# Softmax weights left unscaled until after the product with the values

## The chip, the cores and the metric

The kernel runs on one core of a Trainium2 chip. The metric is the device time of one launch in microseconds. Every operand is fp32.

## The reference, cut to what matters

Two small transformer models run one after the other on 256 tokens of width 1024, each with two layers. The change lies in the first model. Each of its layers projects the 256 tokens and 256 context tokens to queries, keys and values of 16 heads of 64 channels: 8 plain heads ("a", two key heads shared by four query heads each), 4 neighbourhood heads ("b", with a window and a bias on the token keys) and 4 differential heads ("c"). The token queries attend to 512 keys (tokens and context); in layer 0 the context queries also attend, to the 256 context keys. For a and b

```python
p = jax.nn.softmax(s, axis=-1)
out = p @ v
```

and for c, with two maps of scores for each head, half the channels each,

```python
p = jax.nn.softmax(s, axis=-1)
w = p[:, :, 0] - lam * p[:, :, 1]
out = rms_norm(w @ v, g_sub) * (1.0 - lam_init)
```

An output projection, a gated residual and a convolutional feed-forward network follow; then the second model, with attentions of its own that the change doesn't touch.

## The kernel before, in words

All matrix products with weights (`gemm`, `mm`, `mm1`, lines 265 to 303) split both operands into a rounded part and a rest (`weight`, lines 254 to 263, by ScalarE and VectorE; `split`, lines 305 to 307, called by `parts`) and take three products. Activations are kept with channels on the 128 partitions and tokens on the free axis, so a tile of 128 channels holds two heads.

`first_layer` (line 606) runs, in each of the two layers, eight attentions of two heads each: two of kind c, two of kind b, four of kind a (lines 683 to 694). `attend` (line 518) does one. For each of the two heads it takes steps: two steps for the two blocks of 128 token queries, with a score tile of 128 x 512, and, in layer 0 only (`with_ctx`), one step for both blocks of context queries, whose two halves of 256 keys share one tile. In a step `scores` (line 524) fills a PSUM tile from the matmul pool (five banks); kind c fills two, one for each map. `weigh` (line 484) makes weights of them: `soft` (line 473) takes the negated row maximum on VectorE (line 478) and the exponential with that bias on ScalarE, which also gives the row sum (line 480); then VectorE takes the reciprocal of the sum (line 488), and ScalarE multiplies the weights by it, row by row, as the scale of a copy (line 491). For kind c the second map goes through `soft` too, and VectorE adds it to the first, scaled by lambda over its sum (lines 494 to 498). TensorE transposes the four blocks of weights into a PSUM tile of the other pool (three banks; lines 551 and 569), VectorE copies them to SBUF (lines 554 and 572), and after both heads the products with the values sum up the output, 64 channels of each head on its half of the partitions (lines 579 and 586). Here queries lie on the free axis and channels on the partitions, so that a factor for each query would have to lie along the free axis.

The output, still in PSUM, is split by `parts` (ScalarE line 306, VectorE line 307) for the output projection, for kind c after a norm (`subln`, lines 589 to 598).

Between the weights and their transposes each step calls `fill` (line 399), which puts in one tile of the projections still to be done (twelve tiles in each layer: in layer 0 the attentions of kind c use them up, in layer 1 the next ones use the last of them) or, after these, one step of the modulation weights' products (line 372).

The order of the instructions on each engine is fixed before the run by a planner, which takes the program's order as priority and puts an instruction forward where it expects its engine to be free and its inputs ready; buffers of a pool are handed out in that order. At run time each engine works its own list in order and waits at semaphores. The temporaries of 128 x 544 (`self.t`) are a pool of nine, the small columns (`self.s`) one of sixteen.

## Time and profile before

| | before |
|---|---|
| runs shown, median (lowest to highest) | 2435.0 us (2427.2 to 2436.84) |
| the profiled execution's own time | 2433.39 us |
| its span in the profile | 2431.6 us |
| mean granted clock of TensorE | 0.98 of full |
| TensorE products busy | 2320.8 us |
| VectorE busy | 1523.2 us |
| ScalarE busy | 1270.2 us |

All of the profile's numbers come from that one execution; 1.8 us of its time lie around the span. Times in the profile count from the span's start. Engines are PE (TensorE's products), PEld (its weight loads, which overlap the products), DVE (VectorE), ACT (ScalarE), POOL (GpSimd) and SP (SyncE). A busy TensorE isn't TensorE at its peak, since products overlap in its pipeline. "n_t<-at_t" names the tiles that an instruction writes and reads: `mm_t` and `at_t` are the two PSUM pools, `t_t` temporaries, `s_t` small columns, `n_t` activations, `q_t` queries, keys and values. A group may be followed by the idle time of its engine just before it and by the instruction that ended most of that.

### The profile page before, as it was taken

The page shows a single profiled execution, that of the slowest core. Times are in us where ns is not written, and L with a number is a line of the kernel's source. Part 1 is how long each engine was busy: PE and PEld are TensorE (multiplying, and loading weights), DVE is VectorE, ACT ScalarE, POOL GpSimd, SP SyncE. Part 2 cuts the span into 40 slices and gives each one's busy share as a digit, 9 for nine tenths or more (in the row PEclk, how much of TensorE's full clock was granted, in tenths as well). Part 3 has the DMA queues.
Part 4 walks back from the last instruction along what each step waited for, and adds up shares of the span by engine and source line. Part 5 has one row for each costly group of instructions (what it writes and reads, how often), then busy time and mean ns, then how long its engine had stood idle before and what let it go on. Part 6 is the DMA issues. An engine that isn't in the chain of part 4 may idle for free. (4 is left out here: it accounts for less than half of the span.)

```text
span 2431.6 us, 40872 instructions
## 1 busy us (share of the span) xinstructions
PE 2320.8 (95%) x16128; PEld 2043.5 (84%) x16128; DVE 1523.2 (63%) x2605; ACT 1270.2 (52%) x2196; POOL 401.7 (17%) x417
## 2 busy tenths in 40 slices
PE   5999999999999989999999999899999999998998
PEld 3665677778877758999999988899989999888997
DVE  4667665444547776776664876676466557666664
ACT  3658644333346775664444545554454444466553
POOL 0300021000022001211111320321121122113111
PEclk8999999999999999999999999999999999999999
DMA  7313335433233246556555533445545545334653
GB/s 269 103 37 131 113 130 173 139 121 96 93 117 120 71 156 211 194 177 191 183 168 180 167 106 105 148 157 174 174 148 178 169 147 195 104 114 149 196 180 118
DMA packets 100993, 358.57 MB, mean 147 GB/s; under 512 B 11488, under 2 KB 12864, under 8 KB 100544
## 3 DMA queue, kind: packets, MB, share of 16 engines
q1 hardware_dynamic: 98640, 349.82, 44.4%
q0 software_dynamic: 1792, 5.53, 0.9%
q8 instruction: 127, 2.08, 0.4%
q10 hardware_dynamic: 368, 0.59, 0.1%
q14 instruction: 66, 0.54, 0.1%
HBM read 354.83 MB, written 1.07 MB: 146 GB/s over the span
## 5 line engine op out<-in xcount | busy, mean ns | idle before, releaser
L269 PE MATMUL mm_t<-n_t,hi_t 128*128 128x272 f32 (+2 forms) x3600 | 1112.4, 310 | 25.4 <-ACT n_t L839 18.7
L270 PE MATMUL mm_t<-n_t,hi_t 128*128 128x272 f32 (+2 forms) x3600 | 1109.5, 308 | 6.0 <-DVE n_t L840 5.0
L271 PE MATMUL mm_t<-n_t,lo_t 128*128 128x272 f32 (+2 forms) x3600 | 1106.0, 308 | 1.1 <-DVE lo_t L262 1.1
L262 DVE TENSOR_TENSOR lo_t<-raw_t,hi_t 128x1024 fp32r<-128x1024 f32 (+1 forms) x574 | 713.2, 1246 | 391.2 <-ACT hi_t L261 387.1
L261 ACT ACTIVATE hi_t<-raw_t 128x1024 fp32r<-128x1024 f32 (+1 forms) x574 | 595.5, 1039 | 680.6 <-PE mm_t L270 509.4
L269 PEld LDWEIGHTS mm_t<-n_t,hi_t 128*128 128x128 f32 x3600 | 686.0, 191 | 77.7 <-ACT n_t L839 20.9
L270 PEld LDWEIGHTS mm_t<-n_t,hi_t 128*128 128x128 f32 x3600 | 688.5, 191 | 38.1 <-DVE n_t L840 8.4
L271 PEld LDWEIGHTS mm_t<-n_t,lo_t 128*128 128x128 f32 x3600 | 687.9, 191 | 33.0 <-issue 5.8
L269 PE MATMUL mm_t<-q_t,hi_t 128*128 128x272 f32 (+2 forms) x896 | 274.6, 307 | 0.7 <-ACT q_t L306 0.7
L270 PE MATMUL mm_t<-q_t,hi_t 128*128 128x272 f32 (+2 forms) x896 | 274.4, 306 | 0.0
L271 PE MATMUL mm_t<-q_t,lo_t 128*128 128x272 f32 (+2 forms) x896 | 274.3, 306 | 0.0
L343 POOL TENSOR_TENSOR t_t<-t_t 128x272 f32<-128x272 f32 (+1 forms) x108 | 122.9, 1143 | 540.2 <-ACT t_t L339 515.2
L269 PEld LDWEIGHTS mm_t<-q_t,hi_t 128*128 128x128 f32 x896 | 168.4, 188 | 8.8 <-ACT q_t L306 1.1
L270 PEld LDWEIGHTS mm_t<-q_t,hi_t 128*128 128x128 f32 x896 | 168.9, 188 | 7.6 <-DVE q_t L307 0.2
L271 PEld LDWEIGHTS mm_t<-q_t,lo_t 128*128 128x128 f32 x896 | 168.9, 189 | 7.5
L888 POOL TENSOR_TENSOR t_t<-t_t 128x272 f32<-128x272 f32 (+1 forms) x88 | 75.6, 860 | 443.3 <-DVE t_t L882 386.9
L738 POOL TENSOR_TENSOR t_t<-t_t 128x512 f32<-128x512 f32 (+1 forms) x44 | 56.7, 1288 | 442.2 <-ACT t_t L737 442.2
L882 DVE TENSOR_TENSOR t_t<-mm_t,t_t 128x272 f32<-128x272 f32 (+1 forms) x176 | 75.6, 436 | 64.2 <-PE mm_t L271 62.4
L372 PE MATMUL at_t<-raw_t,CS 128*32 128x256 f32 x768 | 70.6, 431 | 35.7 <-DMA raw_t<-in_w_ada_dram 35.4
L307 DVE TENSOR_TENSOR q_t<-t_t,q_t 128x272 fp32r<-128x272 f32 (+2 forms) x112 | 55.8, 498 | 73.4 <-ACT q_t L306 73.4
L306 ACT ACTIVATE q_t<-t_t 128x272 fp32r<-128x272 f32 (+2 forms) x112 | 52.3, 467 | 90.4 <-POOL t_t L738 47.8
L480 ACT ACTIVATE t_t<-mm_t,s_t 128x512 f32<-128x512 f32 (+1 forms) x120 | 72.7, 607 | 26.5 <-DVE s_t L478 25.7
(253 smaller groups left out, 2146.9 us busy)
## 6 DMA issues: line engine op xcount, KB each, us to landing
raw_t<-in_w_up_dram SPq DMA_DIRECT2D x264, 512.0 KB, 3.3
raw_t<-in_w_in_dram SPq DMA_DIRECT2D x118, 512.0 KB, 3.4
raw_t<-in_w_ada_dram SPq DMA_DIRECT2D x96, 512.0 KB, 4.4
raw_t<-in_w_dn_dram SPq DMA_DIRECT2D x96, 448.0 KB, 3.3
raw_t<-in_w_dn_dram SPq DMA_DIRECT2D x48, 512.0 KB, 3.6
raw_t<-in_w_out_dram SPq DMA_DIRECT2D x32, 512.0 KB, 3.4
raw_t<-in_w_fg_dram SPq DMA_DIRECT2D x16, 512.0 KB, 3.3
q_t<-cum POOLq DMA_DIRECT2D x8, 272.0 KB, 7.4
```

Source lines behind the costliest of these rows:

```text
L261: nc.scalar.activation(hi[:, :k], raw[:, :k], AF.Copy)
L262: nc.vector.tensor_tensor(lo[:, :k], raw[:, :k], hi[:, :k].bitcast(F32), ALU.subtract)
L269: self.nc.tensor.matmul(ps, wh, xh, start=start, stop=False)
L270: self.nc.tensor.matmul(ps, wh, xl, start=False, stop=False)
L271: self.last_mm = self.nc.tensor.matmul(ps, wl, xh, start=False, stop=stop).ins
L307: self.nc.vector.tensor_tensor(lo, src, hi.bitcast(F32), ALU.subtract)
L343: st.eng.tensor_tensor(st.acc, st.acc, sq, ALU.add)
L372: self.last_ada = nc.tensor.matmul(ps[32 * g:32 * g + 32], self.CS[:, k, :], wv[:, g], start=k == 0, stop=k == KC - 1).ins
L480: nc.scalar.activation(pm[:, i * nk:(i + 1) * nk], sp[:, i * nk:(i + 1) * nk], AF.Exp, bias=m[:, i:i + 1], accum_out=sm[:, i:i + 1])
L738: nc.gpsimd.tensor_tensor(u, u, g, ALU.mult)
L882: nc.vector.tensor_tensor(u, ps, z[0], ALU.mult)
L888: nc.gpsimd.tensor_tensor(u, u, g, ALU.mult)
```

## The change

The weights are no longer scaled in a step. A tile of eight columns, `sums`, collects the row sums of all steps of an attention: four for each head, the first two for the token queries, the others for the context queries. Kind c scales the second map by lambda times the first map's sum over the second's, so that the first map's sum stays as a common factor. After the steps of both heads VectorE takes the reciprocals (two instructions), and TensorE lays them along the free axis: for each block of 128 queries and each head a product of the column, repeated 64 times as weights, with the identity puts the reciprocals of 128 queries on the 64 partitions of that head, in one PSUM tile of the matmul pool. ScalarE copies that tile to SBUF, and after the products with the values VectorE multiplies the output with it into a temporary, which goes on to `parts` or `subln` in place of the PSUM tile. The second model's attention (`fox`) is as before.

```diff
--- before.py
+++ after.py
@@ -470,32 +470,30 @@
         self.evac(o[:, :n], tp[:, :n])
         return o
 
-    def soft(self, sp, nseg, nk):
+    def soft(self, sp, nseg, nk, sm):
 
         nc = self.nc
         pm = self.t()
-        m, sm = self.s(nseg), self.s(nseg)
+        m = self.s(nseg)
         nc.vector.tensor_reduce(m, sp.rearrange("p (s k) -> p s k", s=nseg), AX.X, ALU.max, negate=True)
         for i in range(nseg):
             nc.scalar.activation(pm[:, i * nk:(i + 1) * nk], sp[:, i * nk:(i + 1) * nk], AF.Exp, bias=m[:, i:i + 1],
                                  accum_out=sm[:, i:i + 1])
-        return pm, sm
-
-    def weigh(self, sps, nseg, nk, lam):
-
-        nc = self.nc
-        pm, sm = self.soft(sps[0], nseg, nk)
-        nc.vector.reciprocal(sm, sm)
-        for i in range(nseg):
-            u = slice(i * nk, (i + 1) * nk)
-            nc.scalar.activation(pm[:, u], pm[:, u], AF.Copy, scale=sm[:, i:i + 1])
+        return pm
+
+    def weigh(self, sps, nseg, nk, lam, sm):
+
+
+        nc = self.nc
+        pm = self.soft(sps[0], nseg, nk, sm)
         if len(sps) == 2:
-            pm1, sm1 = self.soft(sps[1], nseg, nk)
-            nc.vector.reciprocal(sm1, sm1)
-            nc.vector.tensor_scalar(sm1, sm1, lam, None, ALU.mult)
+            f = self.s(nseg)
+            pm1 = self.soft(sps[1], nseg, nk, f)
+            nc.vector.reciprocal(f, f)
+            nc.vector.scalar_tensor_tensor(f, f, lam, sm, ALU.mult, ALU.mult)
             for i in range(nseg):
                 u = slice(i * nk, (i + 1) * nk)
-                nc.vector.scalar_tensor_tensor(pm[:, u], pm1[:, u], sm1[:, i:i + 1], pm[:, u], ALU.mult, ALU.add)
+                nc.vector.scalar_tensor_tensor(pm[:, u], pm1[:, u], f[:, i:i + 1], pm[:, u], ALU.mult, ALU.add)
         return pm
 
     def stack(self, o, n, keys):
@@ -520,6 +518,9 @@
         nc = self.nc
         ident = self.con("ident")
         pts = []
+
+        sums = self.s(8)
+        nq = 4 if with_ctx else 2
 
         def scores(sp, hh, i, qs, ks, last):
 
@@ -544,7 +545,7 @@
                             nc.tensor.matmul(sp[:, rr * P:(rr + 1) * P], self.con("rev"), bias(qi, rr, hh), start=False,
                                              stop=rr == 1)
                     sps.append(sp)
-                pm = self.weigh(sps, 1, 512, lam)
+                pm = self.weigh(sps, 1, 512, lam, sums[:, 4 * hh + qi:4 * hh + qi + 1])
                 self.fill(l)
                 tp = self.atp()
                 for kc in range(4):
@@ -561,7 +562,7 @@
                         scores(sp[:, qi * 256:(qi + 1) * 256], hh, i, slice(256 + qi * P, 256 + (qi + 1) * P),
                                slice(256, 512), True)
                     sps.append(sp)
-                pm = self.weigh(sps, 2, 256, lam)
+                pm = self.weigh(sps, 2, 256, lam, sums[:, 4 * hh + 2:4 * hh + 4])
                 self.fill(l)
                 tp = self.atp()
                 for kc in range(2):
@@ -571,6 +572,16 @@
                 pcx = self.n()
                 nc.vector.tensor_copy(pcx, tp)
             pts.append((px, pcx))
+        for hh in range(2):
+            nc.vector.reciprocal(sums[:, 4 * hh:4 * hh + nq], sums[:, 4 * hh:4 * hh + nq])
+
+        rb = self.mmp()
+        for i in range(nq):
+            for hh in range(2):
+                nc.tensor.matmul(rb[64 * hh:64 * hh + 64, i * P:(i + 1) * P],
+                                 sums[:, 4 * hh + i:4 * hh + i + 1].to_broadcast([P, 64]), ident, start=i == 0, stop=i == nq - 1)
+        rs = self.t()[:, :nq * P]
+        nc.scalar.activation(rs, rb[:, :nq * P], AF.Copy)
         po = self.atp()
         for kc in range(4):
             for hh, (px, pcx) in enumerate(pts):
@@ -584,7 +595,9 @@
                     r0 = 64 * hh
                     vv = v[:, (2 + kc) * P + r0:(2 + kc) * P + r0 + 64]
                     nc.tensor.matmul(po[r0:r0 + 64, 256:512], vv, pcx[:, kc * 256:(kc + 1) * 256], start=False, stop=kc == 1)
-        return po[:, :512 if with_ctx else 256]
+        o = self.t()[:, :nq * P]
+        nc.vector.tensor_tensor(o, po[:, :nq * P], rs, ALU.mult)
+        return o
 
     def subln(self, po, n, gain):
         nc = self.nc
```

## Rows read from the trace of the kernel before

**Rows 1.** Page, part 1: busy us, share of the span, instructions of each engine.

```profile
PE 2320.8 (95%) x16128; PEld 2043.5 (84%) x16128; DVE 1523.2 (63%) x2605; ACT 1270.2 (52%) x2196; POOL 401.7 (17%) x417
```

**Rows 2.** Busy time by stretch: start:end, length, then each engine's us (instructions).

```profile
core 0: us, PE busy (x) PEld busy (x) DVE busy (x) ACT busy (x) POOL busy (x), PEclk, DMA share, GB/s
82.00:202.00 120.00, 112.37 (x506) 77.33 (x505) 81.45 (x167) 78.12 (x160) 21.39 (x24) 0.99 0.17 49
202.00:284.00 82.00, 73.87 (x551) 44.63 (x550) 66.33 (x156) 72.93 (x172) 1.41 (x2) 0.98 0.52 180
284.00:300.00 16.00, 16.00 (x91) 12.21 (x92) 5.71 (x15) 5.23 (x14) 0.00 (x0) 1.00 0.00 2
760.00:833.00 73.00, 67.77 (x360) 48.32 (x359) 54.80 (x114) 50.41 (x100) 17.61 (x19) 1.00 0.30 94
833.00:870.00 37.00, 31.39 (x226) 25.43 (x225) 26.10 (x69) 31.97 (x72) 5.68 (x8) 0.91 0.09 26
870.00:918.00 48.00, 47.42 (x345) 30.35 (x346) 33.78 (x90) 30.66 (x65) 0.00 (x0) 0.99 0.63 211
```

**Rows 3.** The same view of the first two attentions after the differential ones.

```profile
202.00:238.40 36.40, 32.80 (x271) 20.12 (x269) 29.00 (x67) 35.23 (x81) 1.41 (x2) 1.00 0.57 203
```

**Rows 4.** The same view, of line 491 alone.

```profile
core 0: us, ACT busy (x), PEclk, DMA share, GB/s
...
202.00:284.00 82.00, 24.03 (x42) 0.98 0.52 180
...
833.00:870.00 37.00, 4.94 (x7) 0.91 0.09 26
870.00:918.00 48.00, 11.97 (x17) 0.99 0.63 211
```

**Rows 5.** Timeline, 267.5 to 270.7 us: start, length, instruction [idle before, releaser].

```profile
267.53 0.68 ACT L480 ACTIVATE t_t<-mm_t,s_t 128x512 f32<-128x512 f32 x1
...
268.40 0.68 DVE L307 TENSOR_TENSOR n_t<-at_t,n_t 128x512 fp32r<-128x512 f32 x1
...
269.00 0.74 DVE L554 COPY n_t<-at_t 128x256 f32<-128x256 f32 x2
...
269.66 0.15 DVE L488 RECIPROCAL s_t<-s_t 128x1 f32<-128x1 f32 x1
...
269.85 0.72 ACT L491 ACTIVATE t_t<-t_t,s_t 128x512 f32<-128x512 f32 x1 [1.54 <-DVE s_t L488]
...
270.62 0.66 PE L551 MATMUL at_t<-CON,t_t 128*128 128x128 f32 x4 [1.53 <-ACT t_t L491]
```

**Rows 6.** Groups by form, whole span: busy us, mean ns | idle before, releasers.

```profile
L491 ACT ACTIVATE t_t<-t_t,s_t 128x512 f32<-128x512 f32 x64 | 45.2, 717 | 15.8 <-DVE s_t L488 15.6
...
L491 ACT ACTIVATE t_t<-t_t,s_t 128x256 f32<-128x256 f32 x32 | 14.6, 502 | 4.0 <-DVE s_t L488 3.9
...
L551 PEld LDWEIGHTS at_t<-CON,t_t 128*128 128x128 f32 x256 | 30.6, 146 | 21.0 <-ACT t_t L491 10.6 <-issue 7.5 <-ACT t_t L480 0.8
...
L579 PE MATMUL at_t<-n_t,q_t 128*64 128x256 f32 x256 | 36.6, 387 | 1.7 <-DVE n_t L554 1.3 <-DVE q_t L359 0.3
...
L544 PE MATMUL mm_t<-n_t,CON 128*128 128x128 f32 x64 | 9.9, 274 | 0.0
```

**Rows 7.** Timeline of TensorE, 264.2 us.

```profile
264.18 1.95 PE L579 MATMUL at_t<-n_t,q_t 128*64 128x256 f32 x16
```

**Rows 8.** Groups by form, 870 to 918 us.

```profile
L491 ACT ACTIVATE t_t<-t_t,s_t 128x512 f32<-128x512 f32 x17 | 12.0, 719 | 6.1 <-DVE s_t L488 5.9
...
L307 DVE TENSOR_TENSOR n_t<-at_t,n_t 128x256 fp32r<-128x256 f32 x5 | 2.1, 422 | 5.8 <-ACT n_t L306 5.8
...
L306 ACT ACTIVATE n_t<-at_t 128x256 fp32r<-128x256 f32 x5 | 1.9, 383 | 7.2 <-PE at_t L579 7.2
```

**Rows 9.** Groups by form, ScalarE, 202 to 284 us.

```profile
L306 ACT ACTIVATE n_t<-at_t 128x512 fp32r<-128x512 f32 x4 | 2.4, 592 | 1.3 <-PE at_t L586 1.3
```

## The prediction

> **What bounds the kernel now.** I read the page's engine shares first [rows 1]. Over the whole span TensorE has 95% busy, VectorE 63% and ScalarE 52%, which looks as if work taken off ScalarE could buy nothing. But the shares are an average, and all that the diff touches lies in the first model's two attention stages. So the second view is the busy time by stretch [rows 2]: layer 0's differential attentions (82 to 202 us), its neighbourhood and plain attentions (202 to 284), its end under the output projection (284 to 300), and for layer 1 the same at 760 to 833, 833 to 870 and 870 to 918. The reader should see two stretches in which ScalarE is the fuller of the two elementwise engines: 72.93 of 82 us (89%) at 202 to 284, and 31.97 of 37 (86%) at 833 to 870. In the first two attentions of the former it is 35.23 of 36.4 us, 97% [rows 3]. In the stretches of the differential attentions projections run between the steps and TensorE has 94 and 93% [rows 2]; there ScalarE has a third of its time free. At 284 to 300 TensorE has no gap at all.
>
> The third view is the scaling instruction by itself [rows 4]: 24.03 us of ScalarE at 202 to 284, 4.94 at 833 to 870, 11.97 at 870 to 918; the remaining 18.9 of its 59.8 us (45.2 + 14.6, [rows 6]) lie where TensorE is nearly full. The fourth is one step in order of time [rows 5]. The exponential ends at 268.21; its reciprocal is queued on VectorE behind a subtraction and two copies and starts at 269.66; the scaling runs 269.85 to 270.57; the transposes start at 270.62, and TensorE has stood idle for 1.53 us. So the detour sits in the chain of every step, and costs its own 0.15 and 0.72 us plus a place in VectorE's queue. Over the kernel ScalarE idles 19.5 us (15.6 + 3.9) for that reciprocal, and the weight loads of the four-block transposes 10.6 us for the scaling [rows 6].
>
> **What is removed.** The 96 scalings go: 64 of 512 columns at 717 ns and 32 of 256 at 502 ns [rows 6]. So do 80 reciprocals (6 in each attention of layer 0, 4 in layer 1) at 0.15 us [rows 5], 12.0 us of VectorE; I share them out over the stretches as the scalings are. In the differential attentions the second sum's reciprocal stays, and the small multiply by lambda becomes a small multiply by lambda and the first sum, 20 for 20. I cost that at nothing, because the operand that it adds, the first map's sum, is there before the second map's.
>
> **What is added, per attention (16).** (1) Two reciprocals of four or two columns, 0.15 us each like the others: 32, 4.8 us. (2) Broadcast products: 8 in layer 0, 4 in layer 1, 96 in all, 128 columns moving, 64 output rows, two row halves. No row shows one. The nearest is the product with the values, also 64 wide, with 256 columns: 16 take 1.95 us back to back [rows 7], 0.122 each, so half the columns give 0.061, 5.9 us in all. The other end is 0.274 us, a 128-column product by its whole duration [rows 6], 26 us in all. I take 0.061, because these too come in alternating halves. (3) One ScalarE copy out of PSUM, 0.383 us at 256 columns and 0.592 at 512 by the first split, which reads the same kind of tile [rows 8, 9]: 7.8 us. (4) One VectorE multiply, 0.68 us at 512 columns [rows 5] and 0.42 at 256 [rows 8], by the second split: 8.8 us. (5) One more tile of the five matmul banks and two more of the nine temporaries for a few us; as the temporary of every step falls free one scaling sooner, I cost it at nothing. Nothing moves on SyncE's or GpSimd's queue, and no DMA is added.
>
> So ScalarE loses 52.0 us net, VectorE gains 1.6 (8.8 + 4.8 - 12.0), TensorE gains 5.9.
>
> **The sum, by stretch.** *202 to 284* (five attentions end in it). ScalarE: 72.93 - 24.03 + 5 x 0.59 = 51.9 us. VectorE: 66.33 - 4.8 + 10 x 0.15 + 5 x 0.68 = 66.4. VectorE becomes the fuller one. If the stretch runs at the 89% that its fullest engine reaches now, it takes 66.4 / 0.89 = 74.6 us: 7.4 gained. Ends: at the 97% of [rows 3], 68.5 us, 13.5 gained; if VectorE stays at its present 81%, nothing. I take 7.4, because part of VectorE's idle time is waiting for what comes late as in [rows 5].
> *833 to 870* (one ends). ScalarE 31.97 - 4.94 + 0.38 = 27.4, VectorE 26.10 - 1.0 + 0.3 + 0.42 = 25.8; 27.4 / 0.864 = 31.7: 5.3 gained, between 0 and 8.8 (at 97%).
> *870 to 918* (five end). Neither engine is full (30.66 and 33.78 of 48), so only the chain shortens. ScalarE idles 5.9 us there ahead of its 17 scalings [rows 8]; I take half, 3, between 0 and 5.9.
> *82 to 202 and 760 to 833* (two end in each). TensorE's idle time is 7.6 and 5.2 us, which are the upper ends; 0 is the lower. What is removed lies beside projections; I take 1.5 each.
> *284 to 300* (one ends). TensorE is full: 0 gained.
> Gross gain 18.7 us. The broadcast products cost nothing at 202 to 284 and 833 to 870, where TensorE has gaps; elsewhere there are 52 of them (16, 8, 8 and 20), 3.2 us at 0.061, at most 14.2 at 0.274. At a layer's end the last output gets one VectorE operation more (0.42 to 0.68 us), but its last step is shorter by reciprocal and scaling (0.87): nothing.
>
> Net 15.5 us, from the profiled execution's own 2433.39 us: 2418. The median of the runs shown, 2435.0, is 1.6 us above it, so I predict **2420 us**.
>
> TensorE's room at 202 to 284 has to be judged against its 90% busy there, which would leave 8.1 us. Rows speak for more: the products with the values last 387 ns each [rows 6], yet 16 end within 1.95 us [rows 7], so their busy times overlap in a pipeline. The Trainium skill (Perfetto Trace Analysis, Identifying the Most-Contended Engine) calls the matmul row's share a poor measure and judges TensorE by the busy share of weight loads, here 44.63 of 82 us, 54% [rows 2]; by the matmul row the gain at 202 to 284 would be held to 8.1 us, by the weight loads it would not. My term of 7.4 stands by either.
>
> **The rivals.** *A, VectorE only takes ScalarE's place.* For it: VectorE is at 81% already, and its load doesn't fall (66.4 after, 66.3 before). Against it: the waits of [rows 5]. Then 202 to 284 gains nothing, 833 to 870 gains 2, 870 to 918 gains 2 and the rest 1; less 3.2 that is 1.8, some 2433 us.
> *B, more than forecast.* Both full stretches reach 97% (22.3 us), the chain at 870 to 918 gives all 5.9 and TensorE's gaps in the differential stretches close by half (6.4): 34.6 less 3.2, 2404 us. For it: one engine alone would be near full instead of two. Against it: no stretch longer than that of [rows 3] runs so.
> *C, slower: the output multiply blocks VectorE's queue.* At 870 to 918 ScalarE's first split waits 7.2 us in 5 places for the last product, 1.4 each, and VectorE's second split 5.8 us in 5 for ScalarE's, 1.2 each [rows 8]. After the change VectorE itself stands before the products, with the next attention's maxima and copies behind it, and then once more before the split. 16 attentions times 1.4 are 23 us; with 1.2 more, 42. Taken off the gain of 15.5 that gives 2442 to 2461, some 2452 us. It decides from about 1 us of new VectorE idle time per attention (15.5 / 16). Against it: the order of work can put the next attention's steps in between, as it does now.
> *D, the gain isn't there.* If TensorE set the pace throughout, the scalings would be hidden work and only its own 96 new products would count: 2435 + 5.9, 2441 us. For it: 95% in [rows 1]. Against it: the gap of 1.53 us in [rows 5]. The same page of the Trainium skill has the engine of highest occupancy optimised first, TensorE judged by weight loads; over the whole span that is TensorE with 84% [rows 1] and speaks for D; by stretch, as the page has it for kernels of several regimes, it is ScalarE at 202 to 284.
>
> **How the numbers follow.** A measurement of this kernel can tell about 0.5%, 12 us, from no change: faster means below 2423, slower above 2447. Forecast (2412 to 2426) 0.47, A 0.27, B 0.10, C 0.09, D 0.07. Faster: 0.43 of the forecast's 0.47, with B 0.53. Same: the forecast's other 0.04, A 0.27, D 0.06, together 0.37. Slower: C 0.09 and 0.01 of D. The range leaves out C, D and what lies beyond B: 2404 to 2436.
>
> **What would show it.** Right: at the first attentions of layer 0 after the differential ones ScalarE's busy share falls from 89% to below 75% and VectorE's rises above 85%, and they end some 7 us sooner after the differential ones; the transposes are released by the exponential (or, in the differential attentions, by VectorE's addition); the page shows ScalarE near 1218 us and VectorE near 1525. Wrong: if VectorE's idle time ahead of the new multiply sums to over 15 us (C), if VectorE stays at 81% (A), or if the stretches shorten as said but what follows begins no earlier.

## The result, and the profile after

The changed kernel takes **2447.35 us** (median of 5 runs, 2444.42 to 2449.57), the kernel before 2435.0: ratio 1.0057 [1.0041, 1.0074] (with a 95% interval). It got slower by 12 us by the medians and by 14 by the ratio; forecast were 2420 us, between 2404 and 2436. The profiled execution took 2444.42 us, with a span of 2442.6.

Page, part 1, of the kernel after, which answers to [rows 1]:

```profile
PE 2335.7 (96%) x16320; PEld 2055.6 (84%) x16320; DVE 1527.0 (63%) x2573; ACT 1225.0 (50%) x2116; POOL 399.3 (16%) x417
```

ScalarE lost 45 us of work and VectorE gained 4, close to the steps of the prediction. The surprise is in TensorE's count: 192 instructions more, where the prediction had 96 products.

Where the time went is told by how far the kernel had come at a few points. Each is the start of an instruction in the timelines, in us from the span's start; "last value product" is the last product with the values of an attention. The numbers in brackets are against the kernel before. The last column is the run without any scaling (the first experiment below).

| | before | after | removal only |
|---|---|---|---|
| layer 0, last value product, attention 2 | 198.5 | 194.5 (-4.0) | 194.8 (-3.7) |
| layer 0, attention 7 | 283.6 | 283.6 (0) | 268.5 (-15.1) |
| layer 0, attention 8 | 294.0 | 295.6 (+1.6) | 279.7 (-14.3) |
| first load of modulation weights after layer 0 | 314.4 | 320.6 (+6.2) | 301.4 (-13.0) |
| layer 1, attention 2 | 832.2 | 837.1 (+4.9) | 816.6 (-15.6) |
| layer 1, attention 7 | 905.5 | 904.2 (-1.3) | 884.7 (-20.8) |
| layer 1, attention 8 | 916.9 | 920.6 (+3.7) | 894.8 (-22.1) |
| sixth load of feed-forward weights after layer 1's attentions | 945.7 | 956.6 (+10.9) | 926.7 (-19.0) |

After the change layer 0 gains 4.0 us up to attention 2 and has lost them by attention 7, where removal alone gains 11.4 more; layer 1 gains 6.2 from attention 2 to 7. Both layers then lose at their end: from attention 7 to the modulation weights 6.2 us in layer 0, and from attention 7 to the feed-forward weights 12.2 us in layer 1. What follows stays 11 us late to the end (2442.6 against 2431.6 us of span).

Busy time by stretch, kernel after, with the columns of [rows 2] (attentions 3 to 7 of layer 0; then layer 1's attentions 3, 4 to 7, and 8):

```profile
198.00:284.00 86.00, 76.30 (x612) 47.55 (x611) 64.43 (x130) 51.69 (x126) 0.97 (x2) 0.98 0.52 172
...
837.00:862.00 25.00, 22.83 (x174) 20.33 (x172) 16.88 (x45) 18.08 (x44) 4.25 (x6) 1.00 0.08 31
862.00:906.00 44.00, 43.70 (x348) 26.82 (x344) 35.84 (x87) 26.88 (x63) 1.42 (x2) 1.00 0.60 194
906.00:921.00 15.00, 10.76 (x48) 6.92 (x47) 8.12 (x21) 5.34 (x13) 0.00 (x0) 0.66 0.37 133
```

The first row answers to the second of [rows 2]. ScalarE fell from 89% to 60%, as forecast, but VectorE has 75% where over 85% was forecast, and by the table attentions 3 to 7 take 89.1 us where they took 85.1. No engine is full there; TensorE has 89%. The last row is new: at layer 1's end TensorE has 4.2 us without a product, and its granted clock falls.

What the added chain (reciprocals, broadcast products, copy, value products, multiply) looks like in one attention of layer 0, in the timeline of the kernel after:

```profile
263.80 0.17 DVE L576 RECIPROCAL s_t<-s_t 128x4 f32<-128x4 f32 x1
...
264.36 0.38 PE L581 MATMUL mm_t<-CON,s_t 128*64 128x128 f32 x2
...
264.57 0.92 PE L581 MATMUL mm_t<-CON,s_t 128*64 128x128 f32 x11
...
265.71 0.60 ACT L584 ACTIVATE t_t<-mm_t 128x512 f32<-128x512 f32 x1 [1.25 <-PE mm_t L581]
...
266.84 0.69 DVE L599 TENSOR_TENSOR t_t<-at_t,t_t 128x512 f32<-128x512 f32 x1 [0.54 <-PE at_t L597]
...
267.57 0.63 ACT L306 ACTIVATE n_t<-t_t 128x512 fp32r<-128x512 f32 x1 [1.26 <-DVE t_t L599]
```

Each of the three elementwise steps stands at the head of its engine's queue before its input is there. Over the kernel that sums up, in the views of the two lines (who kept the engine waiting: us, times), to 29.2 us of ScalarE before the copy and 20.3 of VectorE before the multiply:

```profile
  PE mm_t L581: 29.2, 10
```

```profile
  PE at_t L597: 11.9, 5
  PE at_t L590: 8.4, 5
```

It is tempting to stop here and call rival C, "the output multiply blocks VectorE's queue", the cause: its sign, over 15 us of VectorE's idle time, is there, and 2447 lies in its range. The experiments leave it a part only.

### The profile page after: what moved, and what is told of

It is laid out like the page before. It is cut to its first block, busy times and chain, and to the rows that moved or that the text cites. A ratio compares the mean times of both kernels' runs of the same rounds, so it can differ in the third digit from the quotient of the medians.

```text
span 2442.6 us, 41159 instructions
## 1 busy us (share of the span) xinstructions
PE 2335.7 (96%) x16320; PEld 2055.6 (84%) x16320; DVE 1527.0 (63%) x2573; ACT 1225.0 (50%) x2116; POOL 399.3 (16%) x417
## 5 line engine op out<-in xcount | busy, mean ns | idle before, releaser
L269 PE MATMUL mm_t<-n_t,hi_t 128*128 128x272 f32 (+2 forms) x3600 | 1112.4, 310 | 25.1 <-ACT n_t L852 18.7
```

The source lines that it names most:

```text
L269: self.nc.tensor.matmul(ps, wh, xh, start=start, stop=False)
```

## The experiments

All ratios are against runs of the kernel before on the same chip. Where terms are compared, a difference of ratios of 0.001 is 2.4 us. The diffs are against the kernel after, if nothing else is said, and `...` marks what is left out of them. The planner lays out each kernel's work anew, so a difference between two kernels also holds what that moved elsewhere; no run takes this out.

**Removal only.** The scalings and their reciprocals go, and nothing takes their place.

```diff
-        for hh in range(2):
-            nc.vector.reciprocal(sums[:, 4 * hh:4 * hh + nq], sums[:, 4 * hh:4 * hh + nq])
...
-        rs = self.t()[:, :nq * P]
-        nc.scalar.activation(rs, rb[:, :nq * P], AF.Copy)
...
-        o = self.t()[:, :nq * P]
-        nc.vector.tensor_tensor(o, po[:, :nq * P], rs, ALU.mult)
-        return o
+        return po[:, :nq * P]
```

> The scalings and their reciprocals go, as in the change, but nothing is put in their place: the reciprocals at the end, the broadcast products, the copy and the multiply by one over the sums are left out, and the output of the attentions stays unscaled. Three theories. T1: the change gains some 4 us per layer in the middle of the attentions and loses some 10 us per layer at their end, because the broadcast takes a matmul bank and the output projection finds none for its first three tiles: then without the broadcast the loss goes too, and this run is 8 to 12 us faster than before, near 2425 us. T2: the same loss, but because the planner, with ScalarE relieved, no longer puts the output projection's products between the last steps: then the loss stays, near 2445 us. U: the loss is the price of the added chain at each attention's end: near 2420 us.

Measured: 2414.59 us, ratio 0.992 [0.9896, 0.9945], so 19 us less, 5 below U's value and 10 below T1's, the nearest two. What bounds attentions 3 to 7 of layer 0 once the scalings are gone, in the busy times of that run from the last value product of attention 2 to that of attention 7:

```profile
194.80:268.50 73.70, 71.91 (x557) 44.29 (x553) 63.12 (x123) 52.31 (x127) 1.41 (x2) 1.00 0.55 186
```

TensorE, with 98% (in the kernel before it has 90% between the same points, 76.4 of 85.1 us). VectorE has 86% and ScalarE 71%.

**Additions only.** The steps scale as before, and the change's additions are made on top, so the output is divided by the sums twice.

```diff
         nc = self.nc
         pm = self.soft(sps[0], nseg, nk, sm)
+        r = self.s(nseg)
+        nc.vector.reciprocal(r, sm)
+        for i in range(nseg):
+            u = slice(i * nk, (i + 1) * nk)
+            nc.scalar.activation(pm[:, u], pm[:, u], AF.Copy, scale=r[:, i:i + 1])
...
-            nc.vector.scalar_tensor_tensor(f, f, lam, sm, ALU.mult, ALU.mult)
+            nc.vector.tensor_scalar(f, f, lam, None, ALU.mult)
```

> Everything that the change adds, but the scaling of the weights stays where it was before (with a reciprocal of its own), so that the output is divided by the sums twice. T1: the output projection loses its banks as in the change and nothing is gained in the middle: 20 us slower than before, near 2455 us. T2: the loss at the end doesn't come, only the additions' own cost: 3 to 6 us slower, near 2440 us. U: slower by more than the change itself, 2450 us or above, and the loss is spread over all attentions, not in the last of each layer.

Measured: 2491.94 us, ratio 1.0241 [1.0217, 1.0264], in U's open range and 37 us above T1's value. The additions cost 59 us beside the scalings; with these gone they cost 33 (2447 less 2414.6). The parts don't add up, so the terms below were all taken from kernels without the scalings.

**The last attention of each layer scaled as before**, the other seven changed.

```diff
-        for hh in range(2):
...
+        if not old:
...
-            O[j] = self.parts(self.attend(l, "a", self.stack(get("qa", j), nq, False), ka, get("va", 0), wc))
+            O[j] = self.parts(self.attend(l, "a", self.stack(get("qa", j), nq, False), ka, get("va", 0), wc, old=j == 3))
```

> The change in all attentions but the last of each layer, which scales its weights as before. T1 and T2: the output projection's products lie between the last steps again and the gain of the middle stays: faster than before, 2425 to 2432 us. U: two of sixteen attentions no longer pay, so seven eighths of the change's 12 us of loss stay: near 2446 us.

Measured: 2434.55 us, ratio 1.0002 [0.999, 1.0014], 3 us above the range of T1 and T2 and 11 below U. The whole loss comes back with two attentions of sixteen.

**The broadcast tile from the other PSUM pool.** One word.

```diff
-        rb = self.mmp()
+        rb = self.atp()
```

> The change with one word altered: the broadcast's PSUM tile comes from the other pool (three banks, of the transposes and outputs) and not from the matmul pool. T1: the output projection has its banks again: 2425 to 2430 us. T2 and U: as the change, 2445 to 2450 us, or a little slower, as the transposes have one bank less for a while.

Measured: 2435.95 us, ratio 1.001 [0.9999, 1.0022], 6 us above T1's range and 9 below that of T2 and U. 11 us come back with all sixteen attentions changed, so it is not the chain behind the last step that the end of a layer pays for, but the pool. TensorE's timeline at the end of layer 1, kernel after:

```profile
904.49 0.50 PE L532 MATMUL mm_t<-q_t 128*128 128x512 f32 x1
...
906.21 0.40 PE L533 MATMUL mm_t<-q_t 128*128 128x512 f32 x1
908.50 0.66 PE L552 MATMUL at_t<-CON,t_t 128*128 128x128 f32 x4 [1.90 <-ACT t_t L480]
909.93 2.06 PE L552 MATMUL at_t<-CON,t_t 128*128 128x128 f32 x8 [0.78 <-ACT t_t L480]
913.56 1.12 PE L552 MATMUL at_t<-CON,t_t 128*128 128x128 f32 x4 [1.56 <-ACT t_t L480]
914.60 0.69 PE L581 MATMUL mm_t<-CON,s_t 128*64 128x128 f32 x2
915.08 1.06 PE L590 MATMUL at_t<-n_t,q_t 128*64 128x256 f32 x2
916.07 0.58 PE L269 MATMUL mm_t<-n_t,hi_t 128*128 128x256 f32 x1
```

and with the tile of the other pool:

```profile
903.20 0.43 PE L581 MATMUL at_t<-CON,s_t 128*64 128x128 f32 x2
903.56 0.38 PE L269 MATMUL mm_t<-n_t,hi_t 128*128 128x256 f32 x1
...
906.99 0.28 PE L270 MATMUL mm_t<-n_t,hi_t 128*128 128x256 f32 x1
907.11 0.28 PE L271 MATMUL mm_t<-n_t,lo_t 128*128 128x256 f32 x1
...
908.19 0.60 PE L552 MATMUL at_t<-CON,t_t 128*128 128x128 f32 x4
908.54 0.36 PE L269 MATMUL mm_t<-n_t,hi_t 128*128 128x256 f32 x1
```

In the second the output projection (lines 269 to 271 on `n_t`) runs between the last attention's steps, as it did in the kernel before:

```profile
907.64 0.28 PE L269 MATMUL mm_t<-n_t,hi_t 128*128 128x256 f32 x1
907.76 0.60 PE L551 MATMUL at_t<-CON,t_t 128*128 128x128 f32 x4
908.11 0.36 PE L270 MATMUL mm_t<-n_t,hi_t 128*128 128x256 f32 x1
```

In the kernel after the four score tiles of the last attention are issued back to back, and TensorE then waits for three exponentials with nothing to put between; the projection begins at 916. Score tiles, broadcast tile and projection all write `mm_t`, a pool of five banks, and four score tiles and a broadcast tile are five. That the pool decides is shown; that it is this count of five is read from these rows and not tried with a sixth bank. The Trainium skill (Perfetto Trace Analysis, Optimization Strategy) says that the same gap coming back on the engine that should be full can mean too little PSUM for the next tile; the three waits of 1.90, 0.78 and 1.56 us agree.

**Multiply only**: a constant tile in place of the copied reciprocals; no reciprocals, no broadcast, no copy.

```diff
-        rb = self.mmp()
...
-        rs = self.t()[:, :nq * P]
-        nc.scalar.activation(rs, rb[:, :nq * P], AF.Copy)
+        rs = self.FIX[:, :nq * P]
...
+        nc.vector.memset(self.FIX, 0.01)
```

> The weights stay unscaled, no reciprocals, no broadcast products and no copy; the output is multiplied by a constant tile, so the factor is not the sum's. Compared with the removal alone (2414.6 us): theory W (VectorE's multiply, waiting at the head of its queue for the last product, is what eats the gain) expects 2430 to 2440; theory V (ScalarE's copy of the broadcast tile is, by its wait for the broadcast products) expects at most 2421, that is VectorE's 8.8 us of multiplies, half of them hidden. If each part only costs its own work, 2419 to 2424.

Measured: 2419.24 us, ratio 0.9936 [0.992, 0.9952], 0.0016 above removal only: 4 us, and by the two intervals not told apart from nothing, but far from the 23 to 42 of rival C. The waits are there all the same (groups by form of this run):

```profile
L590 DVE TENSOR_TENSOR t_t<-at_t,FIX 128x512 f32<-128x512 f32 x8 | 5.5, 686 | 4.2 <-PE at_t L588 4.1
...
L306 ACT ACTIVATE n_t<-t_t 128x512 fp32r<-128x512 f32 x8 | 5.0, 627 | 17.1 <-DVE t_t L590 17.1
```

ScalarE idles 17.1 us before the splits of layer 0 alone, and at most a part of it is in the time. Theory W (the multiply's wait eats the gain) falls for the multiply alone; beside the broadcast it costs more, as the last part of this section shows.

**Broadcast without the multiply**, tile from the other pool; nobody reads the copy.

```diff
-        rb = self.mmp()
+        rb = self.atp()
...
-        o = self.t()[:, :nq * P]
-        nc.vector.tensor_tensor(o, po[:, :nq * P], rs, ALU.mult)
-        return o
+        return po[:, :nq * P]
```

> The weights stay unscaled; reciprocals, broadcast products and the copy are made, the broadcast tile being taken from the three banks of the other PSUM pool; nothing reads the copy, and the output is left unscaled. Theory V expects 2430 to 2437, nearly all that is left between the removal alone (2414.6) and the change with that pool (2436.0); theory W expects at most 2425, about 12 us of own work of the broadcast products, half hidden, and no wait that matters. By both, this run's and the multiply-only run's additions to 2414.6 come to about 21 us together.

Measured: 2427.28 us, ratio 0.9972 [0.9962, 0.9982], 0.0052 above removal only: 12.7 us, under V's 2430 and above W's 2425. Neither theory had it right, and the sum of the two parts (this one and the multiply's 3.9) is 17 us where 21 was expected.

**Both repairs of the layers' ends**, the tile of the other pool and the last attention scaled as before.

```diff
-        rb = self.mmp()
...
+            rb = self.atp()
...
+            O[j] = self.parts(self.attend(l, "a", self.stack(get("qa", j), nq, False), ka, get("va", 0), wc, old=j == 3))
```

> The change, with the broadcast tile from the other pool, and the last attention of each layer scaled in its steps as before. If the bank of the score tiles was all that the last attentions lost (T1), the two repairs are one and the same, and this run comes out like each alone, 2433 to 2437. If the end of a layer also pays for the broadcast, copy and multiply after its last step, which nothing covers, scaling the last attentions gives another 3 to 8 us: 2427 to 2432.

Measured: 2435.17 us, ratio 1.0018 [1.0005, 1.0032]. Like each alone: they repair one and the same thing, and the end pays for nothing else that can be measured.

**A diagonal matrix.** The transposes become products with one over the sums on the diagonal, and all that the change adds after the steps goes.

```diff
+    def diag(self, sm):
+        d = self.t()[:, :P]
+        self.nc.vector.reciprocal(sm, sm)
+        self.nc.vector.tensor_scalar(d, self.con("ident"), sm, None, ALU.mult)
+        return d
...
-                    nc.tensor.transpose(tp[:, kc * P:(kc + 1) * P], pm[:, kc * P:(kc + 1) * P], ident)
+                    nc.tensor.matmul(tp[:, kc * P:(kc + 1) * P], pm[:, kc * P:(kc + 1) * P], dg, start=True, stop=True)
```

> Another way to scale: the weights stay unscaled, and each step's transposes become products with a diagonal matrix of one over the sums, which VectorE makes of the identity (a reciprocal and a multiply of 128 columns, some 0.35 us in a step), so that the output comes out scaled and nothing is added after the steps. If the waits of the added chain (V or W) are what the change loses, this keeps most of the removal's 19 us: 2416 to 2424. If TensorE's instructions set the pace, the 320 further ones of the products (an fp32 product is two where a transpose is one), about 0.05 to 0.1 us each, take 16 to 32 us: 2431 to 2447.

Measured: 2454.12 us, ratio 1.0084 [1.0068, 1.01], slower than either case had it. There is no chain after the steps, ScalarE does even less, and the kernel is 40 us above removal only. What it has more is 320 TensorE instructions, and on VectorE the reciprocals (14.1 us in all) and the multiplies (28.1) ahead of them. The groups of this run show the doubling, 512 where [rows 6] have 256, each weight load 191 ns where it was 146:

```profile
L559 PEld LDWEIGHTS at_t<-t_t 128*128 128x128 f32 x512 | 63.0, 191 | 19.7 <-issue 9.6 <-ACT t_t L480 2.6 <-PE mm_t L539 1.8
```

This led to theory P: after the removal TensorE sets the pace, and the broadcast costs what its instructions take there. The run doesn't show it, for at the 0.064 us an instruction found below 320 of them make half of the 40 us; how much of the rest is VectorE's work stays open.

**Products only**: the broadcast without the multiply and without the copy, tile of the other pool, so that ScalarE has nothing to wait for. The diff is against "broadcast without the multiply".

```diff
-        rs = self.t()[:, :nq * P]
-        nc.scalar.activation(rs, rb[:, :nq * P], AF.Copy)
```

> As the run with reciprocals, broadcast products and copy (2427.3 us), without the copy: the tile of the broadcast products is written and read by nobody, and the output is left unscaled. Theory P (TensorE's own time for the 192 instructions of the products, 12.7 us by that run, 0.066 us each, is the price) expects 2424 to 2428, since only ScalarE's copies of 7.8 us go. Theory V (ScalarE's wait for the products at the head of its queue is the price) expects 2415 to 2419, back near the removal alone, 2414.6.

Measured: 2426.5 us, ratio 0.997 [0.9959, 0.9981], within 1 us of the run with the copy. ScalarE's wait and its copies cost nothing that can be measured here, and V falls. TensorE doesn't wait for the reciprocals either; the view of the products' line has no `L576` among what its engine waited for:

```profile
its engine sat idle before it (us, times) until:
  issue: 5.7, 12
  DVE q_t L359: 2.5, 2
  DVE n_t L555: 2.4, 1
```

**The copy by VectorE**, with the tile of the other pool.

```diff
-        nc.scalar.activation(rs, rb[:, :nq * P], AF.Copy)
+        nc.vector.tensor_copy(rs, rb[:, :nq * P])
```

> The change, with the tile from the other pool, and VectorE copies the broadcast tile in ScalarE's place (7.8 us of ScalarE's work become about 9 us of VectorE's), so that ScalarE never waits for the broadcast products. Theory V expects 2426 to 2431, since the 34.0 us that ScalarE idles ahead of its copy in the run with that pool are the price. Theory P expects 2435 to 2441: the wait only moves to VectorE, which is the fuller engine.

Measured: 2442.72 us, ratio 1.0041 [1.0026, 1.0057], 0.0031 or 7.5 us above ScalarE's copy. V falls here too; a little above P's range. What VectorE does in ScalarE's place isn't free, then; through which wait it costs was not followed.

**Fewer TensorE instructions.** VectorE's reciprocal writes its results 64 times over, and one transpose serves both heads; tile of the other pool.

```diff
+        rep = self.t()[:, :nq * P]
+        nc.vector.reciprocal(rep.rearrange("p (i h c) -> p i h c", i=nq, h=2),
+                             sums.rearrange("p (h i) -> p i h", h=2)[:, :nq].unsqueeze(3).to_broadcast([P, nq, 2, 64]))
...
         for i in range(nq):
-            for hh in range(2):
...
+            nc.tensor.transpose(rb[:, i * P:(i + 1) * P], rep[:, i * P:(i + 1) * P], ident)
```

> The change, with the tile from the other pool, and the broadcast in fewer TensorE instructions: VectorE's reciprocal writes the reciprocals already repeated 64 times (512 columns in layer 0, 256 in layer 1, one instruction in place of two small ones, some 0.4 us more for each attention, 6 us in all), and one transpose for both heads of a block, one instruction, takes the place of two products, four instructions: 48 in place of 192. Theory P expects 144 x 0.066 = 9.5 us less on TensorE, and gives back half of VectorE's 6: 2427 to 2432 against 2436 with that pool. Theory V expects no gain, for ScalarE still waits for the broadcast: 2434 to 2440.

Measured: 2470.43 us, ratio 1.0157 [1.0137, 1.0177]. Both missed, because my price of the reciprocal was wrong by far. Groups by form of this run:

```profile
L576 DVE RECIPROCAL t_t<-s_t 128x512 f32<-128x512 f32 x8 | 26.7, 3343 | 0.0
...
L576 DVE RECIPROCAL t_t<-s_t 128x256 f32<-128x256 f32 x8 | 14.0, 1745 | 0.5 <-ACT t_t L480 0.5
```

A reciprocal of 512 columns takes 3.34 us; I had read 0.15 us off rows of one column [rows 5].

**The same with small reciprocals**, and a VectorE copy that repeats them.

```diff
+        nc.vector.tensor_copy(rep.rearrange("p (i h c) -> p i h c", i=nq, h=2),
+                              sums.rearrange("p (h i) -> p i h", h=2)[:, :nq].unsqueeze(3).to_broadcast([P, nq, 2, 64]))
```

> The run with transposes again, with the two small reciprocals of the change kept and one VectorE copy that repeats the results 64 times (512 or 256 columns, by the other copies at most 0.69 and 0.42 us, 8.9 us in all), because the reciprocals of 512 and 256 columns took 3.34 and 1.75 us there, 40.7 us of VectorE in place of 4.8. The tile is of the other pool, 48 TensorE instructions in place of 192. If the products' instructions are the price (P) and the long reciprocals were what that run lost, 9.5 us go from the 2436 of the change with that pool and half of VectorE's 8.9 comes back: 2429 to 2434. If one more VectorE operation in the chain ahead of the output costs more than the instructions that it saves, 2436 to 2445.

Measured: 2441.39 us, ratio 1.0036 [1.0023, 1.005]: the second case of the expectation, 0.0026 or 6 us slower than 192 instructions were. The view of the transposes' group shows what came in:

```profile
L583 PE MATMUL at_t<-CON,t_t 128*128 128x128 f32 x48 | 8.2, 280 | 7.5 <-DVE t_t L578 7.5
```

TensorE stands 7.5 us before the transposes for VectorE's copy, and 10.2 us before their weight loads in "issue", time for which the profile shows no releaser, where products only had 5.7; in products only it did not wait for VectorE's column at all. So the run doesn't speak on P's price, and how the rest of its loss is made up stays open.

**Products twice**, against products only: 384 instructions in the same places.

```diff
-        for i in range(nq):
+        for i in 2 * list(range(nq)):
```

> As the run with reciprocals and broadcast products alone (2426.5 us against 2414.6 without them), with every product issued twice, 384 TensorE instructions in place of 192; nobody reads the tile, and the output is left unscaled. Theory P (TensorE's own time, 0.062 us for each instruction) expects another 12 us, 2436 to 2441. Theory R (the reciprocals and the place of the products in TensorE's queue, behind the last exponential) expects 2426 to 2430.

Measured: 2435.45 us, ratio 1.0022 [1.0011, 1.0033]. That is 0.0052 or 12.7 us above products only, which were themselves 0.005 or 12.2 us above removal only. The median is half a us below P's range (the kernel before ran 3.5 us faster on this chip than on that of products only), but R's is 5 us away: the price doubles with the instructions. It shows in the stretch where TensorE is full, again from attention 2 to attention 7 of layer 0, first in products only, then in products twice:

```profile
196.90:276.60 79.70, 76.77 (x646) 51.08 (x642) 66.60 (x137) 53.19 (x133) 1.41 (x2) 1.00 0.54 179
...
197.50:282.60 85.10, 82.45 (x719) 55.16 (x716) 66.08 (x135) 52.36 (x132) 1.85 (x2) 0.98 0.53 173
```

The five attentions hold 80 of the 192 instructions. The stretch grows from 73.7 us (removal only) to 79.7 and 85.1, and TensorE's busy time from 71.9 to 76.8 and 82.5; its idle time stays at 2 to 3 us.

**Reciprocals only**, no products; the diff is against products only.

```diff
-        rb = self.atp()
-        for i in range(nq):
-            for hh in range(2):
-                nc.tensor.matmul(rb[64 * hh:64 * hh + 64, i * P:(i + 1) * P],
...
```

> The removal with the 32 small reciprocals, which nobody reads; no products, no copy, no multiply, and the output is left unscaled. Theory P expects 2413 to 2419, near the removal alone (2414.6), VectorE's 5 us at most. Theory R expects 2421 to 2427.

Measured: 2413.01 us, ratio 0.9928 [0.9907, 0.9949], like removal only. R falls and P stands: 192 instructions cost 12.2 us against removal only, 0.064 us each, and 10.2 us (0.0042) against this run, which has the reciprocals too.

**Broadcast without the multiply, tile from the matmul pool.**

```diff
-        o = self.t()[:, :nq * P]
-        nc.vector.tensor_tensor(o, po[:, :nq * P], rs, ALU.mult)
-        return o
+        return po[:, :nq * P]
```

> The run with reciprocals, broadcast products and copy and without the multiply (2427.3 us with the tile from the other pool), with the tile from the matmul pool as in the change; the output is left unscaled. Theory T1 (one of the five banks of the score tiles less is what the layers' ends lose) expects those 11 us again, 2434 to 2441, and the first products of the output projection of layer 1 only after the last score tiles. If the bank only hurts together with the multiply, 2425 to 2431.

Measured: 2446.28 us, ratio 1.0064 [1.0043, 1.0086]: 0.0092 or 22 us above the same kernel with the other pool, twice the 11 expected. The pool alone does it, with no multiply queued behind the tile, and as T1 had it the projection of layer 1 begins only after the last score tiles. The products of line 269 by stretch (busy us and count of products, then of weight loads; granted clock, DMA share, GB/s), here

```profile
900.00:910.00 10.00, 0.00 (x0) 0.00 (x0) 1.00 0.89 285
910.00:920.00 10.00, 1.00 (x2) 0.62 (x2) 0.51 0.37 124
```

in the kernel after

```profile
900.00:910.00 10.00, 0.00 (x0) 0.00 (x0) 0.99 0.83 273
910.00:920.00 10.00, 1.00 (x2) 0.62 (x2) 0.50 0.27 95
```

and in the change with the other pool

```profile
900.00:910.00 10.00, 2.52 (x8) 1.59 (x9) 1.00 0.75 243
910.00:920.00 10.00, 4.29 (x15) 2.88 (x16) 1.00 0.35 107
```

The first two have 2 of these products by 920 us, the third 23. The clock column shows a second cost: where TensorE has waited as in the first two, the granted clock from 910 to 920 us is 0.50 of full (the lower level, 1.2 GHz), and with the projection in between 1.00. In the kernel after it falls during the second of the three waits, after the one of 1.90 us (TensorE's row, busy and clock):

```profile
909.00:910.00 1.00, 0.22 (x3) 0.88 0.51 119
```

A product with the values took 0.38 us in the kernel after at 903.10, and 0.69 at 918.99:

```profile
903.10 0.38 PE L590 MATMUL at_t<-n_t,q_t 128*64 128x256 f32 x1
...
918.99 0.69 PE L590 MATMUL at_t<-n_t,q_t 128*64 128x256 f32 x1
```

How much of the pool's price is clock and how much is waiting wasn't separated.

**What the multiply costs beside the broadcast.** Three pairs of these runs differ in the multiply. It costs 3.9 us alone, 0.0038 or 9.3 us (interval about 4 either way) beside the broadcast with the tile of the other pool, and -1.7 (about 7 either way) beside the broadcast in the matmul pool. With the other pool the copy and the multiply together cost 0.004 or 9.7 us more than products only, and that is clear of noise. The change with the other pool shows where, from attention 2 to attention 7 of layer 0:

```profile
196.30:283.50 87.20, 77.08 (x642) 51.38 (x638) 66.85 (x137) 54.46 (x131) 1.42 (x2) 0.98 0.50 169
```

and in the waits of TensorE there (in total, times, longest), first removal only, then this kernel:

```profile
PE at_t L570 <- ACT t_t L480: 0.8, 1, 0.8
...
PE at_t L552 <- ACT t_t L480: 8.6, 6, 2.0
```

Against removal only the stretch is 13.5 us longer. TensorE's busy time has 5.2 of them, as in products only; its idle time has the other 8.3, up from 1.8 to 10.1, and most of that stands before transposes, for the exponentials of a step. The same waits are 2.1 us in products only and 6.3 in multiply only. So with the multiply the steps' exponentials come too late for TensorE. Which of the queues, VectorE's or ScalarE's, passes the delay on isn't shown by a run.

No version that scales the output beat the kernel before: with the other pool the change comes out level with it, and what remains of the removal's 19 us is spent on the broadcast and on these waits. A sixth bank, a broadcast in another number format, and the change in the attentions of layer 0 alone were not tried.

## Why the prediction was wrong

| term | forecast, us | measured, us | from |
|---|---|---|---|
| scalings and reciprocals go | -18.7, copy and multiply in it | -19.5 | removal only, 0.992 |
| broadcast products | +3.2 | +12.2 | products only less removal only |
| ScalarE's copy | in the first row | +0.5 | with the copy less without |
| output multiply | in the first row | +3.9 | multiply only less removal only |
| all together beyond the parts | 0 | +5.4 | change with other pool less these parts |
| the matmul bank | 0 | +11.4 | change less change with other pool |
| sum | -15.5 | +13.9 | 0.0057 x 2435 |

The measured column is differences of ratios times 2435. The terms for copy and multiply and the fifth row have intervals of some 4 to 8 us about them, and each by itself can't be told from nothing; their sum, 9.7 us, can, and so can the other three. The split depends on the order: from removal only by way of the broadcast in the matmul pool, the same 33 us are 12.7 for products and copy, 22.4 for the pool and -1.7 for the multiply. Only the products' price, 10 to 13 us, hardly moves.

**Right: that the scalings cost time.** The gain came where it was put: by the first table the five attentions at 202 to 284 gained 11.4 us without the scalings (15.1 less 3.7; forecast 7.4, upper end 13.5), and layer 1's attentions 3 to 8 gained 6.5 (22.1 less 15.6; forecast 8.3). The waits of [rows 5] were on the path, and rival D's plain form, "the scalings would be hidden work", is refuted. That 18.7 meets 19.5 is luck in part: the 18.7 have the added reciprocals and multiplies in VectorE's 66.4 us, and without them the same rule gives 61.5 / 0.89 = 69.1 us for that stretch, 12.9 gained there and some 25 in all.

**Wrong: step (5), "One more tile of the five matmul banks ... I cost it at nothing", and "At a layer's end ...: nothing".** I looked at the temporaries and at VectorE's and ScalarE's time behind the last step, and not at who else takes banks of that pool at that moment. [Rows 2] have TensorE full at 284 to 300 and at 47.42 of 48 us at 870 to 918; what filled it at layer 1's end were projection products into the same five banks, as the timeline of the kernel before shows above. The term was 11 us, and 22 without the multiply.

**Wrong: step (2), the broadcast products' price and place.** The instruction's time was right: 0.061 us forecast, 0.064 measured. But [rows 7] counts TensorE instructions, and an fp32 product is two of them; its 16 are 8 products, so 96 products are 192 instructions, 11.7 us by my own row. Measured were 10 to 13. The place was wrong as well: "The broadcast products cost nothing at 202 to 284 and 833 to 870, where TensorE has gaps" holds only while the scalings make the gaps. With them gone TensorE has 98% of the stretch from attention 2 to attention 7, so that the two halves of my sum used the same gap twice. I had VectorE become the fuller engine; it was TensorE.

On that point the prediction weighed TensorE's room. In removal only its matmul row has 98% of that stretch and its weight loads 60% (44.29 of 73.7 us), and 80 instructions more made it 6.0 us longer, 0.075 each. The Trainium skill (Perfetto Trace Analysis, Identifying the Most-Contended Engine) would judge the room by the floating-point work done against the peak, and by the weight loads. The measurement decides for this stretch: the 40% that the weight loads leave free was not there.

**Wrong in part: steps (3) and (4), the copy and the multiply.** They were costed as load on their engines, and the waits that they bring at nothing. With the other pool the two cost 9.7 us, and the trace shows them as idle time of TensorE before the transposes.

**Rival C, a part and not the whole.** Its range holds the result and its sign came up (20.3 us of VectorE's idle time, my bound was 15), and its mechanism is there: beside the broadcast the multiply costs 9.3 us with the other pool, by the interval at most some 13. But it needed 23 to 42, and in the change as it stands the pool costs 11 more. Its decision rule, "about 1 us of new VectorE idle time per attention", took idle time of an engine for time of the kernel: ScalarE's 29.2 us before the copy and VectorE's 20.3 before the multiply go with some 10 us of time.

## What to carry to other kernels

When an edit removes what made an engine wait, work out each added instruction against the engine that is full afterwards, not against the gaps seen before; the gap can be spent once. A new tile of a shared pool has a price at the point where the other users of the pool are what fills the bottleneck, so look there for who takes the next bank, and try the other pool first. And a wait at the head of a queue isn't a price by itself: look for what it holds up on the engine that is full, and put it to a run that takes the wait away, with the rest of the change in place, since the multiply cost 3.9 us alone and 9.3 beside the broadcast.

## What was not expected of the hardware

A VectorE reciprocal of 128 x 512 took 3.34 us and one of 128 x 256 1.75 us, against 0.17 us for 128 x 4; a multiply of 128 x 512 takes 0.69. An fp32 product stands in the trace as two TensorE instructions with a weight load each (192 for the 96 broadcast products), a transpose of fp32 as one (256 for four in each of 64 steps). In the kernel after, TensorE's granted clock fell to 0.50 after a wait of 1.90 us, four transposes and part of a wait of 0.78 us, and stayed there up to 920 us.
